# A list scheduler gets new instruction durations and one time line for VectorE and GpSimd operations with two SBUF operands

## The chip, the cores and the metric

The kernel runs on one core of one Trainium2 chip. The metric is the device time of one execution in microseconds. Three executions of the kernel before took 2767.68, 2771.46 and 2770.51 us; their median is 2770.51 us. Times inside an execution come from one profiled execution.

## The reference

A two-block model at sequence length 1024 and width 1024, in float32. The first block is a mixing layer, a cross-attention on 256 memory rows and a mixture of experts; the second is a gated convolution and a dilated attention. Cut to the order of the work:

```python
# first block
x = x + concat(fourier_mix(u_f), mla_attention(u_q, u_kv, u_kr)) @ w_out   # 8 heads, softmax over 1024 keys
x = x + memory_cross_attention(rms_norm(x), rms_norm(mem))                 # 4 heads, 256 keys
x = x + expert_choice_moe(rms_norm(x))   # 16 experts take their top 128 rows each: silu(a) * b, w_down, gates, scatter-add
# second block, on the normalised rows h2
#   conv part: GLU, a long causal convolution tap by tap, gates z_conv and g_conv, projection yc
#   attention part: q, k, v with rotary embedding, masked local attention in dilated rows, gates z_att and g_att, projection ya
```

## The kernel before

Every product is a split product: a float32 operand is taken apart into a high part (`h`) in a rounded format and a low part (`l`), and three TensorE matmuls stand for one (`xh*wh`, `xl*wh`, `xh*wl`). The high part is a cast on ScalarE (`w2h`, `ks`, `wh`), the low part a subtraction on VectorE, and in some places on GpSimd (`w2l`, `kl`, `wl`). So each weight tile costs one transfer, one ScalarE and one VectorE instruction before TensorE can use it.

Nothing in the program is issued in the order in which it is written. Each call (`k.pe`, `k.act`, `k.dve`, `k.pool`, `k.sp`; class `Rec`) is recorded as an `Op` with the tiles that it reads and writes. `price()` (line 246) gives each a cost, which occupies its engine, and a latency until a user may start. `schedule()` is a greedy list scheduler: it holds a free time for each engine, takes again and again the operation with the earliest possible start (ties go to the one recorded first), gives tiles their slots in SBUF and PSUM, and adds 0.5 us where a result passes to another engine. `issue()` then emits the operations in that order, so that each engine's queue is the scheduler's order cut to that engine. The durations of `price()` decide nothing else: a number that is wrong there shows up as an instruction that stands too early or too late in an in-order queue. All instructions carry the line of the emitting lambda, L180.

Names used further on, all of the second block unless said otherwise. It works through heads two at a time, here called a pair. `q`, `k`, `v` are projections in PSUM. VectorE turns `q` and `k` by the rotary tables: `rt` and `rq` read PSUM and write SBUF, `ro` adds the two. ScalarE casts `qs`, `ks` from `ro`; VectorE forms `kl` from `ro` and `ks`. ScalarE copies `v` to `vf` in two halves; TensorE transposes it into `vt`; ScalarE and VectorE split `vt`. TensorE forms scores `as` from `ks`, `kl` and `qs`; VectorE masks them into `ap` with their row maxima `amx`; ScalarE takes the exponentials; `apt` is the transpose and `ao` the product with `vt`. `z_conv`, `z_att` and `g_conv` are gate projections with no urgent user, which the scheduler puts between as fill. `conv` is the convolution: one VectorE scalar_tensor_tensor for a tap, some taps on GpSimd with a product `ct` from ScalarE. In the mixture of experts, `hg` is the gathered rows, `ht` their transpose, `ea` and `eb` the two hidden products, `sil` their gated product, `gt` its transpose (split into `gth` and `gtl`) and `ey` the expert's output.

Of the kernel before, what the change touches and what calls it, by code (L numbers as in the profile page):

```python
# [67 lines left out]
class V:  # L68


    __slots__ = ("t", "shape", "dt", "chain")
# [73 lines left out]


class Op:
    __slots__ = ("i", "eng", "cost", "lat", "fn", "deps", "tiles", "new", "users", "wait", "ready", "end", "key", "start", "what", "blk", "win", "after", "dma")

    def __init__(self, i, eng, cost, lat, fn):  # L150
        self.i, self.eng, self.cost, self.lat, self.fn = i, eng, cost, lat, fn
# [4 lines left out]
def _psum(v):  # L156
    return isinstance(v, V) and v.t.kind == "pb"


class Rec:  # L160
# [5 lines left out]
    def __getattr__(self, fn):  # L166
        k, eng = self._k, self._eng

        def call(*a, **kw):
            wr, rd = [], []  # L170
            for i, x in enumerate(a):
                if isinstance(x, V):
                    (wr if i == 0 else rd).append(x)
            for n, x in kw.items():
                if isinstance(x, V):
                    (wr if n in ("out", "accum_out") else rd).append(x)

            def issue():
                r = lambda x: x.ap() if isinstance(x, V) else x
                getattr(k.engines[eng], fn)(*[r(x) for x in a], **{n: r(x) for n, x in kw.items()})  # L180

            cost, lat = k.price(eng, fn, a, kw, wr, rd)
            op = k.record(eng, cost, lat, issue, rd, wr)
            return op

        return call


class Program:
# [25 lines left out]
    def record(self, eng, cost, lat, issue, reads, writes):  # L215
        op = Op(len(self.ops), eng, cost, lat, issue)
        op.key = op.i + self.bias
        op.blk = False
        op.dma = 0.0
        op.win = self.win.get(eng, self.win[None]) if not self.far else self.far  # L220
        wt = {id(v.t): v.t for v in writes}
        seen = dict(wt)
        for v in reads:
            t, r = v.t, v.region()
            seen[id(t)] = t
            op.deps.update(i for q, i in t.writers if _overlap(q, r))
            t.readers.append((r, op.i))
        for v in writes:
            t, r = v.t, v.region()
            op.deps.update(i for q, i in t.writers if _overlap(q, r))  # L230
            op.deps.update(i for q, i in t.readers if _overlap(q, r))
            t.writers = [(q, i) for q, i in t.writers if not _within(q, r)] + [(r, op.i)]
            t.readers = [(q, i) for q, i in t.readers if i == op.i or not _within(q, r)]
        op.deps.discard(op.i)
        for t in seen.values():
            if t.first is None:
                t.first = op.i
            t.last = op.i
            t.left += 1
            op.tiles.append(t)  # L240
        op.what = wt and next(iter(wt.values())).name
        self.ops.append(op)
        return op

    def price(self, eng, fn, a, kw, wr, rd):

        out = wr[0] if wr else None
# [5 lines left out]
        if eng == "pe":  # L253
            m = rd[0]
            if fn == "transpose":
                return 0.109 if out.free > 64 or m.shape[0] > 64 else 0.067, 0.06
            n = out.free
            if m.dt in (F32R, BF16):
                return max(n / 2370, 0.109 if m.shape[-1] > 64 else 0.067), 0.06
            return max(4 * n / 2400, 0.2), 0.06  # L260
        ps = any(_psum(x) for x in wr + rd)
        if eng == "act":
            c = n / 1200 + (0.05 if ps else 0.095)
            if any(isinstance(kw.get(q), V) for q in ("scale", "bias")):
                c += 0.045
            if "accum_out" in kw:
                c += 0.05 if n > 256 else 0.0
            return c, 0.05
        if eng == "pool":
            if fn == "tensor_tensor" and any(len(x.shape) > 2 and x.chain and x.chain[-1][0] == "re" for x in wr + rd):  # L270
                return n * 3.1e-3 + 0.07, 0.05
            return n * {"tensor_tensor": 2.19e-3, "memset": 1e-3, "tensor_scalar": 1.01e-3}.get(fn, 3.5e-3) + 0.07, 0.05
        if fn in ("max", "max_index", "match_replace"):
            return 0.66, 0.05
        fast = {"tensor_copy": 1920, "tensor_scalar": 1730, "memset": 1920}.get(fn, 960)
        if ps or not all(len(x.shape) <= 2 for x in wr + rd):
            fast = 960
        if fn == "reciprocal":
            fast = 120
        return n / fast + (0.13 if fn == "scalar_tensor_tensor" else 0.07), 0.05  # L280


    def schedule(self):
        ops = self.ops
        n = len(ops)
# [19 lines left out]
        blocked = []  # L305
        done = np.zeros(n + 1, bool)
        front = near = 0
        order = []

        def allowed(op):  # L310
# [13 lines left out]
        while len(order) < n:  # L324
# [22 lines left out]
            for t in op.new:  # L347
                t.held = True
                s, t.slot, op.after = heapq.heappop(slots[t.kind])
                start = max(start, s)  # L350
                if t.first > front:
                    cnt[t.kind][front:t.first] += 1
            free[e] = start + op.cost
            if op.dma:
                free["sp"] = max(free["sp"], start) + op.dma
# [1673 lines left out]
```

## Time and profile before

| | |
|---|---|
| three runs | 2767.68, 2771.46, 2770.51 us (median 2770.51) |
| profiled execution | 2771.41 us, of which its span 2769.3 us |
| mean granted TensorE clock | 0.979 |
| TensorE matmuls busy | 2659.9 us (96% of the span) |
| VectorE busy | 2096.2 us (76%) |
| ScalarE busy | 1362.1 us (49%) |
| GpSimd busy | 505.6 us (18%) |

The busy times are those of the profile's page. A busy TensorE isn't always one at its peak, since the ends of matmuls are modelled, and a stretch of lower granted clock counts as busy too. The idle time of an engine in a stretch is the stretch less its busy time.

### The profile page before, as it was taken

What the parts mean: (1) busy time and instruction counts of PE and PEld (TensorE: products, weight loads), DVE (VectorE), ACT (ScalarE), POOL (GpSimd) and SP (SyncE); (2) the same over time, 40 slices, a digit from 0 to 9 for tenths busy, and PEclk for the clock granted to TensorE, in tenths of its full rate; (3) what the DMA queues carried; (4) which work ended last, traced back from release to release, by engine and by line L of the source; (5) the groups of instructions that cost most, each with busy time, mean ns of one, the idle gap of its engine ahead of it and who ended that gap; (6) DMA issues with size and microseconds to landing.
All of it is one profiled execution on the core that took longest, in us unless ns stands there. A gap on an engine that the chain in (4) does not pass through costs nothing. (4 is left out here: it accounts for less than half of the span.)

```text
span 2769.3 us, 36068 instructions
## 1 busy us (share of the span) xinstructions
PE 2659.9 (96%) x13230; PEld 2232.0 (81%) x13230; DVE 2096.2 (76%) x3075; ACT 1362.1 (49%) x2177; POOL 505.6 (18%) x270
## 2 busy tenths in 40 slices
PE   8999999999994999999988998999999999999998
PEld 6888888888884888888867877788888888887887
DVE  7367876457567989988978789988889997649553
ACT  6156776333345877777774154534334434524221
POOL 1025555211004200101110133401100002002000
PEclk9999999999996999999999999999999999999999
DMA  4100112545347999999984011212212233449941
GB/s 174 34 34 9 39 54 92 175 154 180 124 139 283 342 358 359 357 356 387 380 302 172 16 61 61 77 54 90 78 42 73 77 137 138 152 164 309 340 173 53
DMA packets 130144, 457.06 MB, mean 165 GB/s; under 512 B 15299, under 2 KB 17539, under 8 KB 129969
## 3 DMA queue, kind: packets, MB, share of 16 engines
q1 hardware_dynamic: 125360, 438.00, 43.7%
q0 software_dynamic: 4608, 16.78, 2.4%
q8 instruction: 104, 1.70, 0.2%
q14 instruction: 72, 0.58, 0.1%
HBM read 378.73 MB, written 69.70 MB: 162 GB/s over the span
## 5 line engine op out<-in xcount | busy, mean ns | idle before, releaser
L180 DVE SCALAR_TENSOR_TENSOR conv<-u,convw,conv 128x1003 f32<-128x1003 f32 (+19 forms) x210 | 298.0, 1426 | 2.2
L180 DVE TENSOR_TENSOR w_upl<-w_up,w_uph 128x1024 fp32r<-128x1024 f32 x128 | 149.2, 1221 | 22.6 <-ACT w_uph L180 21.7
L180 DVE TENSOR_TENSOR w_downl<-w_down,w_downh 128x1024 fp32r<-128x1024 f32 x128 | 149.0, 1222 | 13.3 <-ACT w_downh L180 12.5
L180 DVE TENSOR_TENSOR w_gatel<-w_gate,w_gateh 128x1024 fp32r<-128x1024 f32 x123 | 144.0, 1220 | 7.5 <-ACT w_gateh L180 5.2
L180 ACT CAST w_gateh<-w_gate 128x1024 fp32r<-128x1024 f32 x128 | 125.7, 1057 | 5.7 <-issue 3.3
L180 ACT CAST w2h<-w 128x1024 fp32r<-128x1024 f32 x80 | 83.2, 1050 | 88.9 <-DMA w<-in_w_in_dram 62.1
L180 ACT CAST w_downh<-w_down 128x1024 fp32r<-128x1024 f32 x128 | 126.0, 1054 | 1.4 <-PE ea L180 1.4
L180 ACT CAST w_uph<-w_up 128x1024 fp32r<-128x1024 f32 x128 | 125.7, 1055 | 1.4 <-PE ea L180 0.7
L180 DVE TENSOR_TENSOR w2l<-w,w2h 128x1024 fp32r<-128x1024 f32 x64 | 87.2, 1364 | 37.7 <-ACT w2h L180 19.8
L180 POOL TENSOR_TENSOR wl<-w,wh 128x1024 fp32r<-128x1024 f32 (+3 forms) x31 | 57.3, 1849 | 310.6 <-ACT wh L180 253.3
L180 ACT CAST wh<-w 128x1024 fp32r<-128x1024 f32 (+3 forms) x71 | 62.5, 894 | 78.4 <-DMA w<-in_w_convout_dram 31.6
L180 ACT ACTIVATE ap<-ap,amx 128x128 f32<-128x128 f32 (+1 forms) x192 | 85.5, 449 | 25.5 <-DVE amx L180 25.2
L180 POOL TENSOR_TENSOR conv<-conv,ct 128x1023 f32<-128x1023 f32 (+29 forms) x30 | 74.8, 2493 | 115.5 <-ACT ct L180 115.1
L180 POOL TENSOR_TENSOR w2l<-w,w2h 128x1024 fp32r<-128x1024 f32 x16 | 43.8, 2734 | 263.2 <-ACT w2h L180 208.4
L180 DVE TENSOR_TENSOR ptl<-pt,pth 128x512 fp32r<-128x512 f32 x128 | 81.4, 684 | 8.7 <-ACT pth L180 6.7
L180 ACT ACTIVATE p<-p,mx 128x1024 f32<-128x1024 f32 x64 | 73.8, 1155 | 23.6 <-DVE mx L180 17.3
L180 POOL TENSOR_SCALAR p<-p,sum 128x1024 f32<-128x1024 f32 x64 | 74.2, 1166 | 59.0 <-DVE sum L180 52.7
L180 PE MATMUL eb<-w_uph,hth 128*128 128x512 f32 x256 | 80.5, 394 | 0.1
L1401 POOL DMA_INDIRECT x<-ey,idx x16 | 25.4, 1586 | 302.4 <-ACT ey L180 193.7
L180 PE MATMUL eb<-w_upl,hth 128*128 128x512 f32 x256 | 79.6, 392 | 0.7 <-DVE w_upl L180 0.5
L180 PE MATMUL ea<-w_gateh,hth 128*128 128x512 f32 x256 | 80.1, 393 | 0.0
L180 PE MATMUL ea<-w_gatel,hth 128*128 128x512 f32 x256 | 79.6, 392 | 0.4 <-DVE w_gatel L180 0.4
(554 smaller groups left out, 8663.1 us busy)
## 6 DMA issues: line engine op xcount, KB each, us to landing
w_gate<-in_w_gate_dram SPq DMA_DIRECT2D x128, 512.0 KB, 6.7
w_up<-in_w_up_dram SPq DMA_DIRECT2D x128, 512.0 KB, 6.9
w_down<-in_w_down_dram SPq DMA_DIRECT2D x128, 512.0 KB, 8.1
w<-in_w_in_dram SPq DMA_DIRECT2D x89, 512.0 KB, 4.1
wada<-in_w_adaT_dram SPq DMA_DIRECT2D x24, 512.0 KB, 6.4
convr<-cd SPq DMA_DIRECT2D x16, 512.0 KB, 6.2
amd<-sg SPq DMA_DIRECT2D x16, 512.0 KB, 5.7
ks<-ks SPq DMA_DIRECT2D x24, 256.0 KB, 2.9
```

The source lines that it names most:

```text
L180: getattr(k.engines[eng], fn)(*[r(x) for x in a], **{n: r(x) for n, x in kw.items()})
L1401: self.nc.gpsimd.indirect_dma_start(out=rows.ap(), out_offset=bass.IndirectOffsetOnAxis(ap=idx.ap(), axis=0), in_=x.ap(), in_offset=None, ...
```

## The change

`price()` gets other numbers, and operations that VectorE and GpSimd would run with two SBUF operands (and VectorE's single-source copies between SBUF tiles) are marked by the new `shares()`; `schedule()` lets marked operations of both engines start only when the last scheduled one has ended, on one common clock `port`. No operation is added, dropped or given to another engine. The order changes, and with it the places where ScalarE loads another function table, of which there are 13 in place of 11.

```diff
+            op.port = k.shares(eng, fn, wr, rd)
...
             if fn == "transpose":
-                return 0.109 if out.free > 64 or m.shape[0] > 64 else 0.067, 0.06
+                return 0.11 if out.free > 64 or m.shape[0] > 64 else 0.067, 0.17
             n = out.free
             if m.dt in (F32R, BF16):
-                return max(n / 2370, 0.109 if m.shape[-1] > 64 else 0.067), 0.06
-            return max(4 * n / 2400, 0.2), 0.06
+                return max((n + 32) / 2400, 0.111 if m.shape[-1] > 64 else 0.067), 0.17
+            return max(4 * n / 2300, 0.224), 0.17
...
         if eng == "act":
-            c = n / 1200 + (0.05 if ps else 0.095)
+            c = n / 1200 + (0.055 if ps else 0.095)
             if any(isinstance(kw.get(q), V) for q in ("scale", "bias")):
-                c += 0.045
+                c += 0.1
             if "accum_out" in kw:
-                c += 0.05 if n > 256 else 0.0
-            return c, 0.05
+                c += 0.093
+            return c, 0.105
...
-        return n / fast + (0.13 if fn == "scalar_tensor_tensor" else 0.07), 0.05
+        if any(x.chain and x.chain[-1][0] == "re" and "-> p r i" in x.chain[-1][1] and x.shape[1] > 1 for x in wr + rd):
+            fast = 565
+        c = n / fast + 0.07
+        if fn == "scalar_tensor_tensor" and isinstance(a[2], V):
+            c += 0.065
+        if fn == "stream_shuffle":
+            c += 0.03
+        if "accum_out" in kw:
+            c += 0.08
+        return c, 0.085
+
+    def shares(self, eng, fn, wr, rd):
+        if eng == "pool":
+            return fn in ("tensor_tensor", "tensor_scalar")
+        if eng != "dve" or any(_psum(x) for x in wr + rd):
+            return False
+        big = [x for x in rd if x.free > 8]
+        return len(big) > 1 or fn in ("tensor_scalar", "tensor_copy")
...
+            if op.port:
+                start = max(start, port)
+                port = start + op.cost
             free[e] = start + op.cost
```

Three places show what moves. In a name such as `vf_3268_14842`, the middle number is the tile's, equal in both kernels, and the last an allocation's, which differs. The first place is the second pair of the second block, at 1657 to 1675 us of the trace before. On ScalarE before:

```order
1195 L180 COPY vf_3268_14846<-v_3272_14808 128x4x128
1196 L180 ACTIVATE ct_3273_14851<-u_3139_14051,convw_108 128x1011
1197 L180 CAST ks_3264_14866<-ro_3263_14855 64x1024
1198 L180 CAST ks_3265_14873<-ro_3263_14855 64x1024
1199 L180 COPY vf_3268_14846<-v_3274_14841 128x4x128
1200 L180 ACTIVATE ct_3275_14891<-u_3139_14051,convw_108 128x1010
```

and on ScalarE now:

```order
1200 L180 COPY vf_3268_14842<-v_3272_14807 128x4x128
1201 L180 ACTIVATE ct_3273_14849<-u_3139_14051,convw_108 128x1011
1202 L180 COPY vf_3268_14842<-v_3274_14837 128x4x128
1203 L180 ACTIVATE ct_3275_14882<-u_3139_14051,convw_108 128x1010
1204 L180 CAST vt_3276_14894<-vt_3278_14884 128x4x64 x2
1205 L180 CAST vt_3277_14897<-vt_3279_14889 128x4x64 x2
1206 L180 CAST ks_3264_14901<-ro_3263_14880 64x1024
1207 L180 CAST ks_3265_14905<-ro_3263_14880 64x1024
```

The second half of `vf` no longer stands behind the two casts of `ks`. On VectorE at the same place, before:

```order
1721 L180 TENSOR_TENSOR ro_3263_14855<-rq_3255_14783,rt_3254_14779 128x1024
1722 L180 SCALAR_TENSOR_TENSOR conv_3126_14454<-u_3115_13761,convw_108,conv_3126_14454 128x1015
1723 L180 TENSOR_TENSOR kl_3266_10944<-ro_3263_14855,ks_3264_14866 64x1024
1724 L180 TENSOR_TENSOR kl_3267_10967<-ro_3263_14855,ks_3265_14873 64x1024
1725 L180 SCALAR_TENSOR_TENSOR conv_3126_14454<-u_3115_13761,convw_108,conv_3126_14454 128x1014
1726 L180 TENSOR_TENSOR vt_3276_14904<-vt_3278_14893,vt_3276_14904 128x4x64 x2
```

and now:

```order
1721 L180 TENSOR_TENSOR ro_3263_14880<-rq_3255_14788,rt_3254_14781 128x1024
1722 L180 SCALAR_TENSOR_TENSOR conv_3126_14489<-u_3115_13760,convw_108,conv_3126_14489 128x1015
1723 L180 TENSOR_TENSOR vt_3276_14894<-vt_3278_14884,vt_3276_14894 128x4x64
1724 L180 SCALAR_TENSOR_TENSOR conv_3126_14489<-u_3115_13760,convw_108,conv_3126_14489 128x1014
1725 L180 TENSOR_TENSOR kl_3266_10962<-ro_3263_14880,ks_3264_14901 64x1024
1726 L180 TENSOR_TENSOR kl_3267_10984<-ro_3263_14880,ks_3265_14905 64x1024
```

The same instructions stand between `ro` and the first `ap` of the pair, with one `vt` split and one tap put ahead of the two `kl`.

The second place is the last expert, at 1424 to 1433 us. On VectorE before:

```order
1491 L180 TENSOR_TENSOR sil_2929_13039<-eb_2958_13133,sil_2929_13039 128x512
1492 L180 TENSOR_TENSOR w_downl_2994_13241<-w_down_2992_13199,w_downh_2993_13223 128x1024
1493 L180 TENSOR_TENSOR w_downl_2997_13255<-w_down_2995_13210,w_downh_2996_13233 128x1024
1494 L180 TENSOR_TENSOR gtl_2984_13266<-gt_2985_13239,gth_2983_13257 128x512
1495 L180 TENSOR_TENSOR gtl_2984_13266<-gt_2986_13248,gth_2983_13257 128x512
```

and now:

```order
1491 L180 TENSOR_TENSOR sil_2929_13038<-eb_2958_13137,sil_2929_13038 128x512
1492 L180 TENSOR_TENSOR w_downl_2997_13247<-w_down_2995_13208,w_downh_2996_13233 128x1024
1493 L180 TENSOR_TENSOR w_downl_3000_13261<-w_down_2998_13221,w_downh_2999_13240 128x1024
1494 L180 TENSOR_TENSOR w_downl_3003_13266<-w_down_3001_13228,w_downh_3002_13252 128x1024
1495 L180 TENSOR_TENSOR gtl_2984_13280<-gt_2985_13245,gth_2983_13263 128x512
1496 L180 TENSOR_TENSOR gtl_2984_13280<-gt_2986_13254,gth_2983_13263 128x512
```

Three weight splits stand between `sil` and `gtl` in place of two; `w_downl_2994` has gone ahead of `sil`.

The third place is a later pair, at 2122 to 2131 us. On VectorE before:

```order
2297 L180 SCALAR_TENSOR_TENSOR conv_3437_17802<-u_3423_15857,convw_108,conv_3437_17802 128x1003
2298 L180 TENSOR_TENSOR ro_3807_18516<-rq_3801_18452,rt_3800_18445 128x1024
2299 L180 SCALAR_TENSOR_TENSOR conv_3437_17802<-u_3423_15857,convw_108,conv_3437_17802 128x1002
2300 L180 SCALAR_TENSOR_TENSOR conv_3700_17765<-u_3688_17658,convw_108,conv_3700_17765 128x1011
2301 L180 TENSOR_TENSOR kl_3810_15063<-ro_3807_18516,ks_3808_18527 64x1024
```

and now:

```order
2303 L180 SCALAR_TENSOR_TENSOR conv_3437_17800<-u_3423_15874,convw_108,conv_3437_17800 128x1003
2304 L180 TENSOR_TENSOR ro_3807_18522<-rq_3801_18461,rt_3800_18454 128x1024
2305 L180 SCALAR_TENSOR_TENSOR conv_3437_17800<-u_3423_15874,convw_108,conv_3437_17800 128x1002
2306 L180 SCALAR_TENSOR_TENSOR conv_3700_17765<-u_3688_17658,convw_108,conv_3700_17765 128x1007
2307 L180 TENSOR_TENSOR kl_3810_15075<-ro_3807_18522,ks_3808_18536 64x1024
```

The taps of one convolution are done in falling length: `conv_3700` has come to length 1007 ahead of this `kl`, and had come to 1011, which is four taps more.

## Rows read from the trace of the kernel before

**Rows 1.** The page, busy time of each engine.
```profile
PE 2659.9 (96%) x13230; PEld 2232.0 (81%) x13230; DVE 2096.2 (76%) x3075; ACT 1362.1 (49%) x2177; POOL 505.6 (18%) x270
```

**Rows 2.** Busy by stretch: length, PE, PEld, DVE, ACT, POOL, clock, DMA.
```profile
300.00:400.00 100.00, 98.75 (x637) 87.51 (x636) 81.58 (x199) 70.79 (x126) 51.08 (x35) 1.00 0.15 48
1200.00:1400.00 200.00, 199.27 (x921) 163.66 (x920) 178.17 (x172) 154.16 (x183) 21.70 (x16) 1.00 1.01 376
1600.00:1750.00 150.00, 131.67 (x649) 109.72 (x647) 133.28 (x212) 76.92 (x160) 51.07 (x23) 0.93 0.21 67
...
1663.60:1671.00 7.40, 0.31 (x2) 0.00 (x0) 7.37 (x7) 2.61 (x3) 0.00 (x0) 0.85 0.08 18
...
1680.00:1690.00 10.00, 8.06 (x58) 6.83 (x57) 7.85 (x30) 8.52 (x29) 1.31 (x2) 1.00 0.25 90
...
2100.00:2200.00 100.00, 98.71 (x493) 82.96 (x492) 98.81 (x150) 37.54 (x80) 9.08 (x3) 1.00 0.22 72
```

**Rows 3.** Waits of PE: total us, times, longest us.
```profile
PE vt L180 <- ACT vf L180: 13.4, 5, 7.2
```

**Rows 4.** Time line of ACT at the second pair: start, us, instruction, idle before.
```profile
1668.34 2.11 ACT L180 CAST ks<-ro 64x1024 fp32r<-64x1024 f32 x2 [7.82 <-DVE ro L180]
1670.47 0.58 ACT L180 COPY vf<-v 128x512 f32<-128x512 f32 x1
```

**Rows 5.** Time line of DVE at the second pair.
```profile
1669.42 2.47 DVE L180 TENSOR_TENSOR kl<-ro,ks 64x1024 fp32r<-64x1024 f32 x2
1671.92 1.27 DVE L180 SCALAR_TENSOR_TENSOR conv<-u,convw,conv 128x1014 f32<-128x1014 f32 x1
...
1674.44 0.28 DVE L180 CUSTOM_DVE_ANT_0 ap<-as,mask 128x128 f32<-128x128 f32 x1
```

**Rows 6.** Time line of PE at the second pair.
```profile
1671.11 1.76 PE L180 MATMUL vt<-ident,vf 128*128 128x128 f32 x7 [7.21 <-ACT vf L180]
1672.52 0.46 PE L180 MATMUL as<-ks,qs 128*128 128x128 f32 x1
```

**Rows 7.** Time line of PE at the first pair.
```profile
1603.43 0.66 PE L180 MATMUL vt<-ident,vf 128*128 128x128 f32 x4 [1.45 <-ACT vf L180]
```

**Rows 8.** Time lines of ACT, DVE, POOL and PE at the third pair.
```profile
1736.52 1.13 ACT L180 ACTIVATE ct<-u,convw 128x1003 f32<-128x1003 f32 x1 [8.54 <-DVE ro L180]
...
1738.87 6.24 DVE L180 TENSOR_TENSOR kl<-ro,ks 64x1024 fp32r<-64x1024 f32 x2
...
1737.79 3.33 POOL L180 TENSOR_TENSOR conv<-conv,ct 128x1003 f32<-128x1003 f32 x1 [9.80 <-ACT ct L180]
...
1740.31 1.86 PE L180 MATMUL vt<-ident,vf 128*128 128x128 f32 x8 [3.49 <-ACT vf L180]
```

**Rows 9.** Time lines of PE and DVE in the experts.
```profile
1248.82 0.74 PE L180 MATMUL eb<-w_upl,hth 128*128 128x512 f32 x2 [0.53 <-DVE w_upl L180]
...
1428.24 1.29 DVE L180 TENSOR_TENSOR sil<-eb,sil 128x512 f32<-128x512 f32 x2 [1.51 <-PE eb L180]
1429.45 2.35 DVE L180 TENSOR_TENSOR w_downl<-w_down,w_downh 128x1024 fp32r<-128x1024 f32 x2
...
1432.46 0.73 PE L180 MATMUL ey<-w_downh,gtl 128*128 128x512 f32 x2 [0.94 <-DVE gtl L180]
```

**Rows 10.** Time line of PE at the second block's first norm.
```profile
1464.49 1.11 PE L180 MATMUL h<-ident,x 128*128 128x128 f32 x4 [0.68 <-ACT rb L180]
```

**Rows 11.** Time lines of POOL and DVE at 1594 us, and all `rt`: min/median/max ns.
```profile
1594.74 2.48 POOL L180 TENSOR_TENSOR conv<-conv,ct 128x1019 f32<-128x1019 f32 x1 [3.38 <-ACT ct L180]
...
1594.90 3.40 DVE L180 SCALAR_TENSOR_TENSOR rt<-rt,sin 128x1024 f32<-128x1024 f32 x1
...
L180 DVE SCALAR_TENSOR_TENSOR rt<-rt,sin x24: 1211/1217/3402, 1580.7 to 2393.8; 128x1024 f32<-128x1024 f32 x24
```

**Rows 12.** Time lines of DVE and PE at the pair of 2130 us.
```profile
2127.68 2.46 DVE L180 TENSOR_TENSOR kl<-ro,ks 64x1024 fp32r<-64x1024 f32 x2
...
2130.33 0.27 PE L180 MATMUL as<-kl,qs 128*128 128x128 f32 x1
```

More of the change, by code (lines that the diff above doesn't have):

```diff
@@ L147 @@
 class Op:
-    __slots__ = ("i", "eng", "cost", "lat", "fn", "deps", "tiles", "new", "users", "wait", "ready", "end", "key", "start", "what", "blk", "win", "after", "dma")
+    __slots__ = ("i", "eng", "cost", "lat", "fn", "deps", "tiles", "new", "users", "wait", "ready", "end", "key", "start", "what", "blk", "win", "after", "dma", "port")
     def __init__(self, i, eng, cost, lat, fn):
@@ L218, in record @@
         op.blk = False
+        op.port = False
         op.dma = 0.0
@@ L255, in price @@
             if fn == "transpose":
-                return 0.109 if out.free > 64 or m.shape[0] > 64 else 0.067, 0.06
+                return 0.11 if out.free > 64 or m.shape[0] > 64 else 0.067, 0.17
             n = out.free
             if m.dt in (F32R, BF16):
-                return max(n / 2370, 0.109 if m.shape[-1] > 64 else 0.067), 0.06
-            return max(4 * n / 2400, 0.2), 0.06
+                return max((n + 32) / 2400, 0.111 if m.shape[-1] > 64 else 0.067), 0.17
+            return max(4 * n / 2300, 0.224), 0.17
         ps = any(_psum(x) for x in wr + rd)
         if eng == "act":
-            c = n / 1200 + (0.05 if ps else 0.095)
+            c = n / 1200 + (0.055 if ps else 0.095)
             if any(isinstance(kw.get(q), V) for q in ("scale", "bias")):
-                c += 0.045
+                c += 0.1
             if "accum_out" in kw:
-                c += 0.05 if n > 256 else 0.0
-            return c, 0.05
+                c += 0.093
+            return c, 0.105
         if eng == "pool":
-            if fn == "tensor_tensor" and any(len(x.shape) > 2 and x.chain and x.chain[-1][0] == "re" for x in wr + rd):
-                return n * 3.1e-3 + 0.07, 0.05
-            return n * {"tensor_tensor": 2.19e-3, "memset": 1e-3, "tensor_scalar": 1.01e-3}.get(fn, 3.5e-3) + 0.07, 0.05
+            return n * {"tensor_tensor": 2.19e-3, "memset": 0.85e-3, "tensor_scalar": 1.01e-3}.get(fn, 3.5e-3) + 0.07, 0.05
         if fn in ("max", "max_index", "match_replace"):
-            return 0.66, 0.05
+            return 0.66, 0.085
         fast = {"tensor_copy": 1920, "tensor_scalar": 1730, "memset": 1920}.get(fn, 960)
@@ L307, in schedule @@
         front = near = 0
+        port = 0.0
         order = []
```

## The prediction

> **What bounds the kernel now.** I read the busy times first [rows 1]: TensorE's matmuls fill 2659.9 of 2769.3 us, so a reordering can win at most the 109.4 us that are left, and all of the work of the other engines is cover until TensorE waits for it. Second, the stretches [rows 2], because 96% is an average. In the first attention (300 to 400 us) TensorE lacks 1.25 us of 100, in the experts (1200 to 1400) 0.73 of 200, at 2100 to 2200 1.29 of 100; there it is TensorE that sets the pace. In the first three pairs of the second block (1600 to 1750) it lacks 18.33 us of 150, and VectorE is busy for 133.28: there the chain through VectorE and ScalarE sets it. Third, the waits [rows 3]: `vt` for ScalarE's copy `vf`, 13.4 us in five waits, is the largest that this change can reach. Last the time lines at the places where the order moved.
>
> **What the durations are worth.** The instructions are the same ones on the same engines, so nothing is won or lost in busy time; the change is the sum of waits that go and waits that come. I take the places one by one, in us against the profiled execution.
>
> Second pair, `vf`. Before, ScalarE sits idle for 7.82 us in front of the `ks` casts, which need `ro`, and the second `vf` copy, whose input is long there, stands behind them [rows 4]. TensorE waits 7.21 us for it [rows 6]. Now the copy comes first, and this wait goes. But what is late next is the scores' path: VectorE is busy for 7.37 of these 7.40 us [rows 2], it does the same instructions between `ro` and the first `ap`, only in another order, and so `ap` stays at 1674.44 [rows 5]. `as` could start earlier than 1672.52 [rows 6] only if `kl` were earlier, and it is later by a tap (1.27) and one `vt` split. The wait changes its name, from `vt` to `as`. I count 0; the ends are -7.2 (all of the wait) and +1.6: the tap's 1.27 and one `vt` split, of which four fill the time from the tap's end, 1673.19, to 1674.44, about 0.3 each.
>
> Behind it, from 1680 to 1690, TensorE lacks 1.94 us [rows 2], with small matmuls that wait for the softmax. Now `z_conv` matmuls stand between them, since their weight split comes earlier on VectorE, ahead of the `ap` rows. They come out of a later stretch in which TensorE is the bound. I count the whole, -2.0; the ends are -2.0 and 0.
>
> First pair. The wait of 1.45 for `vf` [rows 7] goes in the same way, and here the scores aren't next, because 22 more `z_conv` matmuls stand ahead of `as`, 4.8 us at 0.22 each (921 of them fill 200 us of the experts [rows 2]). I count -1.4; the ends are -1.5 and, if the fill used here is missed 20 us later, 0.
>
> Third pair. `vt` waits 3.49; `ct` on ScalarE waited 8.54 for VectorE to let go of its buffer, so that the GpSimd tap came at 1737.79 beside `kl`, and the two `kl` took 6.24 [rows 8] against 2.47 for two of them where GpSimd stood still [rows 5]. Now ScalarE does `ct` and both `vf` ahead of the casts and the GpSimd taps start earlier, beside operations of which some read PSUM. Against that, one weight split has gone 50 us back, and the fill that it feeds is missing here, 14 matmuls or 3.1 us. Of the 3.77 us too much of `kl` I take two fifths, -1.5, since the taps meet other VectorE work instead; ends -3.5 (the whole wait) and +1.
>
> Experts. TensorE's idle time in 200 us is 0.73, of which 0.53 is the one wait at 1248.82 for a weight split [rows 2, 9]. The transposes that stood scattered among `ey` now stand in blocks. The idle time alone would give -0.7; matmuls that start late in a row are shown as busy, so I take twice that, -1.5, with ends -3 and 0.
>
> Last expert, the second place of the order. `gtl` stood behind two weight splits (2.35 us) and `ey` waited 0.94 for it [rows 9]. Now there are three behind `sil`; the one moved ahead fits into the 1.51 us that VectorE waited there. One split more is 2.35 / 2 = 1.2, and nothing is left on TensorE to cover it: +1.2, ends 0 and +2.4.
>
> First norm of the second block. `h` waits 0.68 for `rb` [rows 10]. A cast `w2h` now stands ahead of `rb` on ScalarE, and its weights land late. Of the `ks` casts, which are as long per partition, two take 2.11, one 1.05 [rows 4]. That is what the norm loses, and four small matmuls that were put ahead of the next wait hide part: +0.6, ends 0 and +2.
>
> Pair of 2130 us, the third place. The second `kl` ends at 2130.14 and `as` with the first starts at 2130.33 [rows 12]; the first `kl` was there half of 2.46 earlier, so the slack is 2130.33 - 2128.91 = 1.4. Four taps more stand ahead, 4 x 1.27 = 5.1 [rows 5], in a stretch where VectorE is busy for 98.81 of 100 [rows 2]; TensorE has four matmuls, 0.9 us, more ahead of `as`. That would make TensorE wait 5.1 - 1.4 - 0.9 = 2.8. Since some of the taps may fill waits of VectorE further up I take +2.0; ends 0 and +2.8.
>
> First attention and the front: the `s` tiles come 3 to 4 us earlier against VectorE, fill goes behind them, and a 3 us subtraction moves into the softmax. These offset each other, as far as I can follow them: 0, ends -3 and +3. The two table loads fall where ScalarE waits: 0.
>
> The sum is 0 - 2.0 - 1.4 - 1.5 - 1.5 + 1.2 + 0.6 + 2.0 + 0 = -2.6. The profiled execution took 2771.4 and would take 2768.8. It lies 0.9 above the median of the three runs, so the runs should show **2768**.
>
> **The common time line.** Beside a GpSimd tap of 2.48 us that began at 1594.74, `rt` took 3.40, and 1.217 is its median over 24 [rows 11]: the excess of 2.18 is about what the GpSimd instruction still had to run (1597.22 - 1594.90 = 2.32). So VectorE loses the whole time there, and a scheduler that knows it can put an operation that reads PSUM into it, where one is ready.
>
> The Trainium skill ("SBUF — State Buffer", section "SBUF: two separate sides") says that a VectorE operation with two SBUF operands and a GpSimd operation that reads SBUF take the shared ports as an exclusive lock, the later one waiting for the end. The trace agrees (3.40 against 1.217). This speaks against a gain from the line: by the rule the two add up whichever is first, so that spacing them wins nothing by itself and the sum stays at -2.6; were the slowdown only a sharing while both run, spacing would even lose the overlap, 2.48 + 1.217 - 3.40 = 0.3 for a pair of them.
>
> **The rivals.** A: the right durations and the line help wherever VectorE is the bound, and not only at the waits that I could follow. For it speaks the 18.33 us that TensorE lacks in 1600 to 1750, more than six times my sum. Against it, the second pair, where the wait only changes its name. Two thirds of the 18.33 is -12.2 from the median: 2758.
>
> B: the waits change their names nearly everywhere, the second pair being the model, and the order makes no difference: 2770.5. For it speaks that instructions move by a few rows only and the stretches with TensorE at 99% can't give more than 0.7.
>
> C: slower. More convolution taps ahead of `kl`, as in the third place of the order, in five of the later pairs as well, each pair losing the 2.0 of one of them: +10 on top of the sum without that term (-4.6 + 5 x 2.0 + 2.0 = +7.4), 2778. It decides from where the taps ahead of `kl` exceed 2.3 us, the 1.4 of slack and 0.9 of fill. For it speaks VectorE's 98.81 of 100; against it, that TensorE's fill also moved ahead of `as` in most pairs, and that VectorE has no more to do in all.
>
> **How the numbers follow.** Forecast 0.40, A 0.20, B 0.15, C 0.25. The forecast's own range, from the ends of its terms taken together as partly independent, is 2762 to 2774. The range of 8 in 10 reaches towards A and C on both sides, 2755 to 2781. A measurement of this kernel can tell about 0.2% (5.5 us) from no change. Faster by more than that is A's 0.20 and about 0.16 of the forecast's 0.40; slower is most of C and a rest of the forecast, 0.26; within it lies 0.38.
>
> **What would show it.** Right: no wait of `vt` for `vf` above 2 us, but an idle time of TensorE of some 5 us ahead of `as` in the second pair; TensorE's idle time in 1600 to 1750 down by 3 to 6 us; `ey` waiting near 2 us for `gtl` in the last expert; `as` or `kl` among TensorE's waits near 2130. Wrong: that wait gone without one in its place (A), `as` waiting for `kl` in many pairs (C), or a change in the first attention of more than 3 us, which I put at 0.

## The result, and the profile after

| | runs | median us | ratio to before, 95% interval |
|---|---|---|---|
| before | 2767.68 to 2771.84 | 2770.99 | |
| after | 2778.64 to 2790.18 | 2788.8 | 1.0056 [1.0042, 1.007] |

The change makes the kernel slower by half a per cent, some 15 us by the ratio (the medians are 17.8 apart); the forecast was 2768 with a range up to 2781. The profiled execution of after took 2778.64, the shortest of its four; its span of 2776.8 is 7.5 over that of before. The changed kernel profiled again on another chip (run `again`: 2785.94, 1.0052 [1.0038, 1.0066]) has a span of 2784.1 and the same waits. One execution of `busy_in_wait` below took 3840.71 us at a granted clock of 0.65 and is left out of its median.

To see where the time goes I take the same TensorE instruction in two traces and the difference of its start times; the table has the median over 50 us of before's time line. A step from row to row is a loss or a gain in between, apart from what a changed order of the matmuls does to single rows.

| us in before | after | again | durations alone | line alone | new first block | new second block | line, first block |
|---|---|---|---|---|---|---|---|
| 50 | -5.4 | -5.0 | +2.8 | -4.4 | -4.5 | 0.0 | -5.3 |
| 250 | -8.2 | -7.8 | +4.1 | -8.4 | -8.9 | 0.0 | -8.9 |
| 350 | -5.1 | -4.8 | +8.5 | -11.7 | -5.8 | 0.0 | -12.1 |
| 550 | -2.8 | -1.7 | +15.0 | -6.7 | -3.2 | -0.5 | -5.5 |
| 1150 | -3.0 | -0.3 | +16.6 | -5.3 | +1.3 | -0.9 | -4.3 |
| 1350 | -6.3 | -3.6 | +13.3 | -5.3 | -2.0 | -0.9 | -4.3 |
| 1600 | -0.8 | +3.2 | +20.5 | -6.7 | +2.9 | +5.0 | -5.2 |
| 1700 | -5.8 | -1.9 | +19.7 | -7.9 | +3.0 | 0.0 | -6.4 |
| 1750 | +4.3 | +10.9 | +21.9 | +11.7 | +3.9 | +10.1 | -6.4 |
| 1850 | +2.8 | +9.4 | +21.8 | +13.0 | +3.9 | +8.6 | -6.4 |
| 1900 | +8.6 | +15.5 | +22.0 | +38.2 | +3.9 | +14.4 | -6.4 |
| 2350 | +2.5 | +9.5 | +21.5 | +31.4 | +3.8 | +5.6 | -7.4 |
| 2650 | +1.3 | +8.4 | +21.3 | +29.7 | +4.0 | +4.5 | -7.1 |
| 2700 | +7.5 | +14.8 | +27.1 | +31.5 | +4.4 | +12.7 | -7.0 |

After is ahead of before until 1700 us and loses in three places: the third pair (1740 to 1775, +10.1), 1905 to 1925 (+5.8) and the tail (2680 to 2692, +6.2). In between it wins back 1.5 by 1850 and 7.3 from 1925 to 2650, so that 7.5 is left. `again` has 4 us more by 1600 and 2.7 more at the third pair.

The page of after, busy time of each engine, which answers to [rows 1]: there is as much work as before.

```profile
PE 2660.0 (96%) x13230; PEld 2236.4 (81%) x13230; DVE 2096.9 (76%) x3075; ACT 1367.2 (49%) x2179; POOL 494.0 (18%) x270
```

The stretches of [rows 2] in after: length, then busy time of PE, PEld, DVE, ACT and POOL, granted clock, DMA.

```profile
300.00:400.00 100.00, 95.75 (x621) 84.65 (x620) 81.42 (x197) 72.00 (x128) 54.16 (x37) 1.00 0.15 52
1200.00:1400.00 200.00, 200.00 (x931) 166.28 (x930) 179.47 (x174) 156.81 (x185) 20.61 (x16) 1.00 1.00 367
1600.00:1750.00 150.00, 130.69 (x655) 111.94 (x653) 129.65 (x231) 80.64 (x175) 50.37 (x22) 0.90 0.20 64
...
1680.00:1690.00 10.00, 10.00 (x63) 8.73 (x62) 9.54 (x28) 6.75 (x22) 3.87 (x3) 1.00 0.16 54
2100.00:2200.00 100.00, 100.00 (x490) 84.07 (x490) 97.83 (x142) 35.83 (x73) 7.29 (x3) 1.00 0.24 85
```

The experts, 1680 to 1690 and 2100 to 2200 have no idle time of TensorE left. The first attention (300 to 400) has 3.0 us more of it, and 1600 to 1750 has 19.31 in place of 18.33, where I had expected 3 to 6 less.

TensorE's waits in after (total us, times, longest), which answer to [rows 3], cut to those of interest: `vt` for `vf` is gone from the list.

```profile
PE as L180 <- DMA ks<-ks: 14.6, 2, 8.1
...
PE apt L180 <- DVE scratch L180: 4.3, 2, 2.5
PE ya L180 <- DVE attl L180: 4.2, 1, 4.2
PE fo L180 <- ACT mgh L180: 4.1, 1, 4.1
```

In its place stands `as`, two waits with 14.6 us, and what it waits for is a transfer. TensorE in after at the second and the third pair (start, us, instruction, idle before), which answer to [rows 6, 8]; and at the third `kl` on VectorE and the transfer `ks` on SyncE's queue, then that transfer's row in the view of DMA issues (KB each, us to landing):

```profile
1670.35 0.44 PE L180 MATMUL as<-ks,qs 128*128 128x128 f32 x1 [6.50 <-DMA ks<-ks]
...
1737.73 0.45 PE L180 MATMUL as<-ks,qs 128*128 128x128 f32 x1 [8.10 <-DMA ks<-ks]
...
1736.17 2.47 DVE L180 TENSOR_TENSOR kl<-ro,ks 64x1024 fp32r<-64x1024 f32 x2
...
1734.69 1.57 SPq L180 DMA_DIRECT2D ks<-ks  x2
```

```profile
ks<-ks SPq DMA_DIRECT2D x24, 256.0 KB, 2.9
```

`ks` is cast for 64 partitions and handed to the other 64 by a transfer (`self.sp.dma_start(x[i][far] ...)` in `stack_k`). The chain to the scores is `ro`, cast, transfer of 2.9 us, `as`, and not `ro`, cast, `kl`, `as`, as I had it. The two ends lie close together: the first of the two `kl` is through at 1737.40 (half of 2.47 behind 1736.17), 0.3 ahead of the scores.

The clock behind the wait, third pair of after, in stretches of 5 us:

```profile
1730.00:1735.00 5.00, 0.00 (x0) 0.00 (x0) 5.00 (x5) 1.79 (x4) 0.00 (x0) 0.98 0.00 2
1735.00:1740.00 5.00, 2.27 (x11) 2.30 (x11) 4.94 (x10) 0.73 (x1) 0.00 (x0) 0.50 0.46 105
1740.00:1745.00 5.00, 5.00 (x28) 5.00 (x27) 2.75 (x26) 3.86 (x17) 0.00 (x0) 0.50 0.30 108
1745.00:1750.00 5.00, 5.00 (x26) 4.90 (x25) 3.38 (x13) 4.60 (x16) 0.00 (x0) 0.50 0.02 6
1750.00:1755.00 5.00, 4.81 (x25) 3.42 (x24) 3.16 (x6) 3.80 (x9) 0.00 (x0) 0.81 0.27 99
```

A granted clock of 0.50 is the lower level, 1.2 GHz; it stays for three stretches, which begin with the end of an idle time of 8.10, and PE counts as busy in them.

The tail of before and of after, SyncE's queue: `xfr` loads the residual (512 KB each), `amd<-sg` stores the last partial sums and `mg<-amd` reads them back.

```profile
2677.38 0.32 SPq L180 DMA_DIRECT2D amd<-sg  x1
2682.44 0.32 SPq L180 DMA_DIRECT2D mg<-amd  x1
```

```profile
2677.66 1.90 SPq L180 DMA_DIRECT2D xfr<-xf  x3
2679.66 0.40 SPq L180 DMA_DIRECT2D amd<-sg  x1
2688.00 0.32 SPq L180 DMA_DIRECT2D mg<-amd  x1
```

From the store to the read it is 5.06 us before and 8.34 after, where three loads have just been put ahead; `fo` waits 4.08 us for `mgh`, the cast behind it.

### The profile page after: what moved, and what is told of

Its sections match the earlier page's. It is cut to its first block, busy times and chain, and to the rows that moved or that the text cites. A ratio compares the mean times of both kernels' runs of the same rounds, so it can differ in the third digit from the quotient of the medians.

```text
span 2776.8 us, 36042 instructions
## 1 busy us (share of the span) xinstructions
PE 2660.0 (96%) x13230; PEld 2236.4 (81%) x13230; DVE 2096.9 (76%) x3075; ACT 1367.2 (49%) x2179; POOL 494.0 (18%) x270
## 4 chain that ended last, share of the span: by engine, by line
PE 83%; DVE 9%; DMA 3%; ACT 2%; issue 2%; POOL 1%; SPq 0%; DVEq 0%; ACTq 0%; POOLq 0%
PE ea L180 6%; PE ey L180 6%; PE x L180 6%; PE eb L180 6%; PE q L180 5%; PE k L180 4%; PE v L180 4%; PE g_att L180 3%; PE mq L180 3%; PE yc L180 3%; PE glu_a L180 3%; PE fo L180 3%; PE glu_b L180 3%; PE z_conv L180 3%; PE s L180 2%; PE u L180 2%
## 5 line engine op out<-in xcount | busy, mean ns | idle before, releaser
L180 DVE SCALAR_TENSOR_TENSOR conv<-u,convw,conv 128x1003 f32<-128x1003 f32 (+24 forms) x210 | 292.8, 1399 | 2.0
L180 DVE TENSOR_TENSOR w_downl<-w_down,w_downh 128x1024 fp32r<-128x1024 f32 x128 | 149.3, 1217 | 15.2 <-ACT w_downh L180 14.6
L180 ACT CAST wh<-w 128x1024 fp32r<-128x1024 f32 (+3 forms) x71 | 62.5, 897 | 84.9 <-DMA w<-in_w_convout_dram 31.5
L180 DVE TENSOR_TENSOR ptl<-pt,pth 128x512 fp32r<-128x512 f32 x128 | 81.5, 683 | 15.8 <-ACT pth L180 14.8
L180 PE MATMUL ey<-w_downh,gtl 128*128 128x512 f32 x256 | 78.9, 389 | 2.1 <-DVE gtl L180 2.1
```

## The experiments

**The two halves of the change.** `durations_only`: the new `price()` without `op.port`. `line_only`: the old `price()` with `op.port`.

> The new durations without the common time line. Theory (the line pushes the weight split back): w2l_3401 stands where it stood before, so the third pair loses nothing; 2766 to 2773 us, within 0.2% of before, with no wait of `as` above 3 us. Rival (the new durations do the harm, through TensorE's latency of 0.17 in place of 0.06 and the longer ScalarE costs): +0.3 to +0.7%, 2779 to 2790.

> The common time line with the old durations. Theory (the line does the harm): w2l_3401 is late as in the changed kernel, third pair as there, so +0.2 to +0.5%, 2777 to 2785 us, with an `as` wait of 6 to 9 us near 1740. Rival (the durations do it): within 0.2% of before.

Measured: 2798.39, 1.0104 [1.0088, 1.0119], and 2805.43, 1.0126 [1.0111, 1.0142]. Both lie above what either theory allowed. Each half alone is slower than both together, so their parts don't add (1.0231 by the product, 1.0056 measured). The durations lose 20 us in the first block and 5.8 in the tail, but only 2 at the third pair; in the pairs `vt` still waits for `vf` (12.6 us). The line wins 4 to 12 us in the first block and loses 39 in the second, and of the two halves it alone brings the long wait of `as` for `ks` (14.1 us, longest 8.2).

**The blocks.** In `new_first_block` `price()` and `port` are new in the first block and old in the second, in `new_second_block` the other way round, and `line_first_block` has old durations and the line in the first block only:

```diff
+            op.port = k.phase < 4 and k.shares(eng, fn, wr, rd)
```

> New durations and line for what is recorded in the first block, the old ones without the line in the second. Theory (the loss is in the second block; the first block stood 2.2 us ahead of before at its end): 2766 to 2771 us, -0.2 to 0%. Rival (the first block's order, in which attention waits grew by some 5 us, sets the loss in the runs that no trace shows): +0.3% or more, 2779 and up.

> The kernel before in the first block, the new durations and the common time line in the second block only. Theory 1 (the losses at the third pair, at 1910 and at the tail belong to the new order of the second block itself): +8 to +14 on the kernel before, about 2781, with the third pair losing some 10 us between 1740 and 1775, and the `as` wait of 8 us there. Rival (the lag with which the engines enter the second block decides how its waits fall, so that the parts do not add): the third pair keeps its place within 3 us and the total lies within 5 us of the kernel before.

> Old durations everywhere, the common time line only for operations recorded in the first block. Theory (the line helps where TensorE follows the first attention and harms in the second block's pairs; in line_only the first block stood 5 to 6 us ahead of before from 1000 to 1650 us, and lost 46 us between 1700 and 1950): 2762 to 2768 us, -0.1 to -0.3%. Rival (a lead is given back, since a different end of the first block disturbs the second, as in new_first_block): 2769 to 2776.

Measured: 2775.56, 1.0013 [1.0004, 1.0022]; 2781.43, 1.0036 [1.0023, 1.0049]; 2766.79, 0.9981 [0.9972, 0.999]. The first lies between its two theories; the other two came out as their first theory had it. The third pair, 1905 and the tail lose as much with an unchanged first block (+10.1, +5.8 and +8.2): those losses are the second block's own. The line in the first block alone is faster than both kernels of the comparison, and 5 us faster than before.

**Is it the fill, at the third pair?** `third_pair_split_early` moves the weight split `w2l_3401` back ahead of the third pair, so that its `z_conv` matmuls can be done there. They don't come back to their old places, though: in before, four `z_conv` stand between `vt` and the first score and 26 between that and the pair's last `ao`; here it is 40 and none.

```diff
+            if op.what == "w2l_3401":
+                op.key -= 400
```

> The changed kernel, with one operation, the weight split w2l_3401, given the priority of one recorded 400 earlier: it stands on VectorE where it stood before, and 40 matmuls of z_conv stand between vt and the third pair's scores in place of none. Theory (missing fill and the lower clock behind the 8.1 us wait cost 10 to 13 us at the third pair): the shift against before stays near -6 to -2 us past 1760 us, the wait of `as` there falls below 2 us, and the time is 2770 to 2778. Rival (the third pair is bound by VectorE's chain and fill only moves the wait): the shift at 1760 is again +4 or more, 2780 to 2787.

Measured: 2779.69, 1.0026 [1.0017, 1.0035], but the third pair loses 13.1 us (-0.8 to +12.3). TensorE at its first scores, and the clock:

```profile
1749.37 0.44 PE L180 MATMUL as<-ks,qs 128*128 128x128 f32 x1 [4.72 <-DMA ks<-ks]
```

```profile
1750.00:1755.00 5.00, 5.00 (x28) 5.00 (x27) 2.88 (x19) 3.26 (x16) 0.00 (x0) 0.50 0.17 47
```

The fill shortens the wait (4.72 for 8.10), but measured from the lag with which the kernel enters the pair (-0.8; after -5.8) the first score comes 6.6 us later than in after. SyncE's queue has the larger part of that: a weight load `w` of 512 KB now stands ahead of the transfer.

```profile
1743.55 0.33 SPq L180 DMA_DIRECT2D w<-in_w_in_dram  x1
1743.99 1.11 SPq L180 DMA_DIRECT2D ks<-ks  x2
```

The transfer goes out 1.3 us behind the end of its cast, and the scores start 5.4 us after it; in after these two are 0.0 and 3.0. VectorE's `ro` (1738.52) has 1.8 of the rest. So this run takes the missing fill away and puts another loss in its place, and doesn't tell what the fill alone costs. What this kernel gains it gains at 1905 and in the tail.

**Is it the half clock?** `busy_in_wait` puts spare matmuls into the two waits, into the scores' own PSUM tile ahead of the real ones (`n` is 24 in the second pair and 32 in the third, `w` is `qs`); all other instructions keep their order.

```diff
+            for _ in range(n):
+                self.engines["pe"].matmul(out.ap(), w[:, :P].ap(), w[:, :512 if len(out.shape) == 2 else P * out.shape[1]].ap(), start=True, stop=True)
```

> The changed kernel, with work on TensorE in its two long waits for the ks transfer and nothing else altered: 24 spare matmuls of 512 columns ahead of the first `as` of the second pair (24 x 0.228 = 5.5 us in a wait of 6.5) and 32 ahead of that of the third (7.3 us in a wait of 8.1); they write the scores' PSUM tile, which the real matmul then overwrites. The order of all other instructions stays. Theory 1 (a wait costs a second time, in the half clock that the profile shows behind it): the granted clock stays at 1.0 where it was 0.50 from 1670 to 1677 and from 1737 to 1751, the `as` waits fall to about 1 us each, and half of those 3 + 13 us comes back where TensorE is what is waited for: 4 to 9 us less than the changed kernel's 2786 to 2789, about 2780. Rival (behind the wait the softmax chain through VectorE and ScalarE sets the pace, so the clock does not matter): the clock stays up, the time stays within 2 us of the changed kernel's.

Measured: 2782.07, 1.0032 [1.002, 1.0045]. The clock stays up, and the third pair still loses 10.1 us (0.0 to +10.1):

```profile
1735.23 7.53 PE L1727 MATMUL as<-qs 128*128 128x512 f32 x32
1743.78 0.30 PE L180 MATMUL as<-ks,qs 128*128 128x128 f32 x1 [1.02 <-DMA ks<-ks]
1746.67 0.33 PE L180 MATMUL apt<-ident,ap 128*128 128x128 f32 x1 [0.92 <-DVE amx L180]
```

```profile
1740.00:1745.00 5.00, 3.98 (x24) 3.20 (x23) 4.94 (x6) 1.75 (x2) 0.00 (x0) 1.00 0.46 105
1745.00:1750.00 5.00, 3.75 (x31) 3.23 (x30) 3.83 (x30) 3.88 (x18) 0.00 (x0) 1.00 0.28 105
1750.00:1755.00 5.00, 3.75 (x23) 2.90 (x23) 3.86 (x13) 4.97 (x19) 0.00 (x0) 1.00 0.33 102
```

What the matmuls gain at the full clock they wait for the softmax: of the 10 us from 1745 on TensorE is idle for 2.50. At the pair the rival was right; the profiled execution (2785.16) is within 1 us of `again`, the median some 4 below it. `line_first_block_busy` does the same (34 and 11 spare matmuls ahead of `vt`) in the two waits for `vf` that the second block of before keeps:

> The common time line in the first block only (2766.8 alone, durations of before), and spare matmuls on TensorE in the two long waits for `vf` that the second block of before keeps: 34 of 384 columns (5.8 us in a wait of 7.2) in the second pair, 11 of 512 columns (2.5 us in a wait of 3.5) in the third. Theory 1 (the half clock behind a wait costs TensorE's time): the clock stays at 1.0 from 1665 to 1674, where it was 0.50 to 0.68, and from 1735 to 1740, where it was 0.69; 3 to 5.5 us less, about 2762.5, the fastest of all. Rival (the softmax chain sets the pace there): 2765 to 2768.

Measured: 2768.03, 0.9991 [0.9982, 1.0], against 2766.79 without them: the rival again. Both runs keep the clock up in a wait of a pair and nowhere else.

**Is it a buffer?** VectorE does two `ro` in a pair, that of `q` and some 16 us later that of `k`. With the same VectorE instructions ahead of it (but one split), the third pair's `ro` of `k` comes 64.2 us after a fixed tap of the second pair in after and 62.5 in before, and 8.6 us of that are idle in after, 5.0 in before. Two waits make up the difference in idle time, one at `rq` and one at the `ro` of `q`:

```profile
1703.67 0.69 DVE L180 SCALAR_TENSOR_TENSOR rq<-q,cos 128x512 f32<-128x512 f32 x1 [1.39 <-POOL conv L180]
...
1715.88 2.05 DVE L180 TENSOR_TENSOR ro<-rq,rt 128x1024 f32<-128x1024 f32 x1 [2.27 <-PE k L180]
```

This `ro` reads nothing that TensorE's `k` matmuls write. The planner has 50 buffers for tiles of this size. As I read its order, a shuffle `rt` of `k`, which before stands behind this `ro`, now stands ahead of it and takes the last free one, and `ro` gets that of the `k` weights, which the matmuls still read. `ro_other_buffer` records `rt` and `rq` of `k` as depending on the `ro` of `q` (its number is in `k.ro3`):

```diff
+            if eng == "dve" and op.what in ("rt_3345", "rq_3346"):
+                op.deps.add(k.ro3)
```

> The changed kernel, in whose third pair the shuffle `rt` and the product `rq` of the k projection are recorded as depending on `ro` of the q projection. In the changed kernel they stand ahead of it and take the last free page, so that `ro` gets the page of the k weights and VectorE stands still for 2.27 us until TensorE's k matmuls are through (1715.88, released by `k`); now `ro` takes the page of a finished tap, and a tap of the convolution fills the time. Theory 1 (the third pair is late because VectorE's chain is: its idle time between the second pair's scores and the third `ro` is 8.63 us against 5.04 before): VectorE's wait of 2.27 goes, the `as` wait of 8.1 falls by 1 to 2.3 us, the third pair loses 8 to 9 us instead of 10 to 13, and the time falls by 1 to 4 us. Rival (the page is beside the point, the wait of 8.1 is set by the fill that TensorE has already used up): the `as` wait stays at 8 and so does the time, 2784 to 2789.

Measured: 2780.15, 1.0036 [1.0022, 1.0049]. VectorE's wait of 2.27 is gone, which bears the reading out, and the wait of `as` is down by 1.7:

```profile
1718.50 2.04 DVE L180 TENSOR_TENSOR ro<-rq,rt 128x1024 f32<-128x1024 f32 x1
...
1740.45 0.44 PE L180 MATMUL as<-ks,qs 128*128 128x128 f32 x1 [6.35 <-DMA ks<-ks]
```

But the pair loses 10.2 us (-1.3 to +8.9), as before the mend; against `again` the time comes back at 1905 (about 2 us) and in the tail (about 3). With a better-placed buffer the wait is shorter and the loss isn't.

**VectorE's order.** `chain_first` puts the VectorE and ScalarE steps of this pair's `q` and `k` 200 places ahead, so that six taps come behind `ro` instead of ahead.

> The changed kernel, with the VectorE and ScalarE operations of the third pair's `q` and `k` (rt, rq, ro, qs, ks, kl) put 200 places ahead in the planner's order, so that ten taps of the convolution stand ahead of the `ro` of `k` no longer: six of them, 1004 to 1009 elements long, come behind it. TensorE's loss between the same two matmuls of the third pair (time less columns at 2250 per us) is 11.6 us before and 20.1 in the changed kernel, and neither more fill, nor the clock, nor the buffer of `ro` changed it. Theory 1 (VectorE's taps ahead of `ro` make the scores late, the chain on VectorE is what TensorE waits for): six taps of 1.26 are 7.6 us, the `as` wait of 8.1 falls to 1 to 3, the loss to 12 to 15, the time by 4 to 8 us to about 2779. Rival (VectorE must do the taps anyway, and behind the scores they delay the softmax by as much): the `as` wait falls, waits of apt or ao for VectorE take its place, the loss stays at 18 to 21 and the time at 2784 to 2789.

Measured: 2799.58, 1.01 [1.0084, 1.0115], a miss of both theories: the third pair loses 35.4 us by the measure of the expectation, where after loses 20.1. Moved ahead, the two `ro` wait for buffers again, and longer:

```profile
1713.53 4.16 DVE L180 TENSOR_TENSOR ro<-rq,rt 128x1024 f32<-128x1024 f32 x1 [5.55 <-PE z_conv L180]
...
1737.66 1.87 DVE L180 TENSOR_TENSOR ro<-rq,rt 128x1024 f32<-128x1024 f32 x1 [2.20 <-POOL conv L180]
```

With the tail mended as well (`chain_first_last_loads`, expected at 2770 to 2779) it is 2791.41, the 8 us of the tail and no more.

**The tail.** `last_loads_late`: the residual loads but for two wait for the last `amd<-sg` (its number is in `k.last_sum`).

```diff
+            if op.what and op.what.startswith("xfr_") and op.what not in ("xfr_4552", "xfr_4562"):
+                op.deps.add(k.last_sum)
```

> The changed kernel, with the loads of the residual rows (xfr) that stand right ahead of the last store of a gated sum put behind it, so that the round trip amd has the queues for itself. Theory (those three loads of 512 KB lengthen the last round trip from 5.1 to 8.3 us, and fo waits 4.1 to 4.4 us for it and some low clock behind): -3 to -6 us against the changed kernel, 2778 to 2783, with no wait of `fo` for `mgh` above 1.5 us. Rival (the sum itself is late, since three weight splits stand ahead of it on VectorE): -1 to 0 us, and fo still waits over 3 us.

Measured: 2777.89, 1.0022 [1.0013, 1.0031], 8 us below `again`. SyncE's queue:

```profile
2683.66 0.32 SPq L180 DMA_DIRECT2D amd<-sg  x1
2687.52 0.32 SPq L180 DMA_DIRECT2D mg<-amd  x1
2687.89 2.96 SPq L180 DMA_DIRECT2D xfr<-xf  x6
```

Store to read is 3.86 us now, the wait of `fo` is gone, and the lag stays at +6.0 from 2650 to the end. This loss is settled.

> The changed kernel with both mends: the page of `ro` in the third pair as in the run beside it, and the residual loads of the last stage held until the last partial sums are on their way. If the two losses are separate, the gains add: 8 us from the tail (2777.9 alone) and 1 to 4 us from the page, 2774 to 2777, still behind the kernel before. If the time lost in the third pair is only moved along, the tail's 8 us alone: 2777 to 2779.

Measured: 2774.75, 1.0011 [1.0002, 1.002], as expected if the two losses are separate: 3 us below the mend of the tail alone, with single runs from 2767.24 to 2779.59. It is the best that I got out of the new order of the whole kernel, and it is still behind before.

**Two controls.** The kernel before, with 0.52 and with 0.48 us in place of 0.50 for a signal between engines in the planner, and nothing else changed.

> The kernel before with the scheduler's latency between engines 0.52 us in place of 0.50 and nothing else: a change of no physical content, which moves instructions all the same. Theory (before is a lucky draw: its constants were chosen against its own order, and any other order costs some us): +0.2 to +1%, 2776 to 2798 us, by waits at other places than those of the changed kernel. Rival (the loss belongs to the durations and the line): within 0.2% of before, 2765 to 2776.

> The kernel before with one number of its model altered the other way: 0.48 us instead of 0.50 for a signal between engines, no duration and no line altered. Theory 1 (the order of before is the best of many near-equal ones, any other draw of the greedy scheduler is worse by 5 to 25 us): 2776 to 2795, with waits at other places than with 0.52. Rival (with 0.52 it was the direction: the model's signals are too short already and a smaller figure helps or changes nothing): 2765 to 2774.

Measured: 2789.39, 1.0059 [1.0045, 1.0073], and 2795.75, 1.0091 [1.0077, 1.0106]. Either way it is slower by as much as the whole change or more, and for the greater part at other places. With 0.52 it loses 6 us in the first block, nothing at the third pair, 6.6 from 2500 to 2650, where `g_conv` waits 7.1 for `w2l` (5.1 in before), and 5.1 in the tail, where `fo` waits 3.6 for `mgh` as it does in after. With 0.48 it loses 17 to 18 in the first block, 3.5 at the third pair and 4.3 in the tail.

## Why the prediction was wrong

**The step that failed** is the third pair, -1.5 with ends -3.5 and +1, where the runs have +10, and in it the fill: "missing here, 14 matmuls or 3.1 us" by the prediction, and set against nothing but the far end of the range. TensorE's `z_conv` matmuls alone, from 1500 to the start of the pair's last `ao`, before and then after:

```profile
1500.00:1761.14 261.14, 39.50 (x144) 0.96 0.21 71
1500.00:1755.48 255.48, 27.86 (x105) 0.94 0.20 69
```

That is 39 fewer. With two `glu` matmuls more it makes 37, at 0.228 us each 8.4 us; from 1700 to 1850 the table loses 8.6 (-5.8 to +2.8). The parts that I had followed came true and won nothing: the wait of `vt` is gone, and the two `kl` take 2.47 instead of 6.24 [rows 8]. For the chain through VectorE, ScalarE and the transfer is no longer and no shorter than before: after enters the pair 5.8 us ahead, its first score is 5.9 ahead (1737.73 for 1743.67) and its last `ao` 5.7. TensorE is through with `vt` at 1729.63 and then stands idle or has little to do under this chain: between the first score and the last `ao` there are 31 fill matmuls in before and 8 in after. What isn't done there has to be done behind it. I also left the transfer of `ks` out of the chain, although it is in the code; with `kl` through only 0.3 us sooner the number doesn't hang on that.

That the order with the common line costs this is shown: the loss comes with the line alone and the new second block alone, and not with the durations alone or the first block alone. The fill fits the runs: `new_second_block`, `busy_in_wait` and `ro_other_buffer` lack the same 37 matmuls there and lose 10.1, 10.1 and 10.2, whatever the clock and the wait of `as`; `line_first_block` lacks none and loses nothing. `again` lacks 37, and its chain from the first score to the last `ao` is 2.5 us longer than in after; it loses 12.8. `line_only` (42) and `chain_first` (46) lose more than the count, through waits that I didn't follow. But no run puts the fill back at its old places and moves nothing else, so that this last step is counted and not shown by a change of it alone.

**The other terms.** Second pair: the wait changed its name from `vt` to `as` and kept its size (6.50 for 7.21), as forecast, though it ends with the transfer. From 1600 to 1700 after gains 5.0 us; 0, -2.0 and -1.4 make 3.4. The experts gave -3.3 (-1.5 forecast, -3 the end of its range). Last expert: `ey` waits 2.07 for 0.94, +1.1 (+1.2 forecast). First norm: `h` waits 1.49 for 0.68, +0.8 (+0.6 forecast). TensorE's rows of after at these two:

```profile
1428.23 0.72 PE L180 MATMUL ey<-w_downh,gtl 128*128 128x512 f32 x2 [2.07 <-DVE gtl L180]
...
1462.29 1.11 PE L180 MATMUL h<-ident,x 128*128 128x128 f32 x4 [1.49 <-ACT rb L180]
```

The pair at 2130: +2.0 forecast, no wait there. The four taps don't delay `kl`: it starts 4.2 us behind its `ro` (2136.94 and 2132.70), 4.3 in before, with two taps between them in both; the four were done further up. The first attention, counted 0, gives back 5.4 us between 250 and 550 of the 8.2 won before it: more than the 3 us that I had named as the sign of an error.

**What was in no term.** First, 1905 to 1925 (+5.8). `apt` waits 1.79 for VectorE, and the clock falls behind it:

```profile
1918.64 0.41 PE L180 MATMUL apt<-ident,ap 128*128 128x128 f32 x2 [1.79 <-DVE scratch L180]
...
1920.00:1925.00 5.00, 4.97 (x18) 4.51 (x19) 4.94 (x8) 2.96 (x5) 2.31 (x1) 0.50 0.29 112
```

The idle time (1.79 and 0.30 behind it) and some 7 us of work at 0.50, which cost half of that, make 5.6; this is an estimate from the rows, and the place was not tried by itself. Second, a gain: most of the 7.3 won back from 1925 to 2650 lies near 2333, where before has this wait and a clock of 0.50 from 2334 to 2341, and after has neither.

```profile
2333.01 2.34 PE L180 MATMUL cs<-ones,csq 128*128 128x1 f32 x16 [1.48 <-POOL csq L180]
```

Third, the tail (+6.2), a move on SyncE's queue. I had read the order of the compute engines and not asked which transfers of the queue change places.

**The rivals.** A (faster) and B (no difference) are out. C had the direction and, at 2778, nearly the profiled execution's 2778.64, but that is luck, since it had not the place: no run shows taps ahead of `kl` making the later pairs late. On the common line I said that spacing wins nothing. In the first block the order that comes with it is 5 us faster (0.9981), while the new durations are what costs there; whether that is the spacing itself or only another order, no run tells.

**What none of the steps allowed for** is what the controls show: a planner's number moved by 0.02 us, with no reason in the hardware, costs 0.6 to 0.9%. The order of before is one draw of a greedy rule, and the five other draws for the whole kernel (the change, its two halves and the two controls) are all slower. A sum over the waits that I could follow says nothing about the waits that a new draw brings elsewhere.

## What to carry to other kernels

Before believing in a scheduler's new table, change a number of the old one by a trifle and time that, and take the difference as the noise of the method. Where a wait is to go, follow the chain behind it to the end, with every transfer and every buffer that a step must be given. Then count the work that the waiting engine does under that chain in either order: what was missing there came behind it here, at its full price, and a shorter wait or a faster clock changed nothing of that. An order of instructions is also an order of the DMA queue: read that one too, above all at the end of the program, where nothing covers it.

## What the runs showed of the hardware

TensorE's granted clock went to 0.50 in or right behind idle times of 6.5 and 8.1 us and stayed there for some 7 and 14 us of work (second and third pair of after); it also did so, for some 7 us, behind an idle time of 1.79 (after, 1919) and one of 1.48 (before, 2334). Kept at 1.00 by spare matmuls in the waits of the pairs it won nothing: there the chain through VectorE and ScalarE kept its length. The transfer of `ks` (256 KB) took 2.9 us from issue to landing; with a load of 512 KB issued 0.44 us ahead of it the scores started 5.4 us behind its issue, in place of 3.0. Three loads of 512 KB put on the queue just ahead of a store went with 8.34 us from the store to the read of the same data; with these loads held back it was 3.86.
